# The opening of a conditioned decoder trunk: loads, folded products and the condition's spread in another order

## The chip, the cores and the metric

The kernel runs on one core of a Trainium2 chip. The core has five engines that run their own instruction streams and wait for each other by semaphores: TensorE (PE in the profile, with its weight loads as PEld), VectorE (DVE), ScalarE (ACT), GpSimd (POOL) and SyncE (SP), whose queue issues most DMAs here. The metric is the device time of one execution in microseconds (us); lower is better.

## The reference

The reference is a trunk of two layers on `x` (1 x 1024 x 1024, f32) with a condition vector `c` (1024 numbers). Each sub-layer is RMSNorm, a shift and a scale made from `c`, a mixer, a gate made from `c`, and the residual sum. The first layer's mixer projects to 2 x 2048 channels, takes trailing means over 2, 4, 8 and 16 positions minus the input, multiplies each of four groups of 512 channels by its own matrix, gates and projects back:

```python
def pool_mixer(h, w_in, w_group, scale, w_out):
    u, z = jnp.split(h @ w_in, 2, axis=-1)
    p = causal_multiscale_pool(u).reshape(B, S, N_POOL_GROUPS, GROUP_WIDTH)
    y = jnp.einsum('bsgc,gcd->bsgd', p, w_group).reshape(B, S, A_WIDTH) * scale
    return (y * jax.nn.silu(z)) @ w_out

for l in range(DEPTH):
    shift, scale, gate = jnp.split(silu(c) @ ada_w[l] + ada_b[l], 3, axis=-1)
    h = modulate(rmsnorm(x, norm_g[l]), shift, scale)
    y = mixer(h, ...)            # pooling in layer 0, windowed attention in layer 1
    x = x + gate[:, None, :] * y
return rmsnorm(x, final_g)
```

The second layer is grouped-query attention over a window of 128 positions with a shared key and value. Only the opening of the first layer is touched by the change.

## The kernel before, in words

Every f32 matrix product is made from two rounded parts of each factor, a high part (`fp32r` copy) and a low part (the factor minus its high part), in three passes: high x high, high x low, low x high. So a 128x128 by 128x512 product is three matmuls.

`x` lies transposed in SBUF as eight row blocks of 128 channels, `xk[0..7]`, each in two halves of 512 positions (`q` = 0, 1). The opening is written out by hand: inside `tc.manual_schedule` every engine runs its instructions in the order of the code. It does these things side by side:

- **Folded products** (`join_mm`, L306). For the first group the input projection and the group matrix are multiplied together first: eight blocks `m` (0 to 7), each a sum over four chunks `ci`. `fetch_c(ci)` loads the chunk's two matrices (`wgr`, and `raw` for the weights `wu`). `split_wg` makes high and low parts of `wgr` (high on ACT, L291; low on POOL, L292) and `split_wu` those of `raw` (high on ACT, low on DVE, L299 and L300). `raw` has two buffers, so the load of chunk 2 waits on SP until `split_wu(0)` is done, and that of chunk 3 until `split_wu(1)` is. Six of the eight blocks are summed in the banks `d`, `d`, `d`, `d`, `S`, `S`; blocks 6 and 7 follow in the two `S` banks once blocks 4 and 5 have left them. `joined_h` (ACT, L311) and `joined_l` (DVE, L316) turn the sums into parts.
- **Condition.** `c` lands in one row of `cact`. A product with a row of ones spreads it over 128 partitions (L434, banks `tp` and `o`); tanh on ACT (L437) and a multiply on DVE (L439) make the SiLU. `dots(k, i)` (`ada_dot`, L238) are DVE multiply-and-sum instructions: one column of shift (i = 0) or scale (i = 1) for row block `k`, from a 512 KB tile that `fetch_ada(k)` (L287) loads. There are two pairs of such tiles; `k` runs 0, 4, 1, 5, 2, 6, 3, 7.
- **Statistics.** `squares(q, ...)` on ACT (L387) and `adds(q, ...)` on DVE (L392), `fold`, then `rstd_stats` on PE: matmuls of one column (L161), `v` on DVE (L164), a power on POOL (L166), and `rstd_spread` (PE, L173), which ACT copies to `rbs[q]`.
- **First product.** `first_h(k, q)` (DVE L353, then ACT L355) and `first_l(k, q)` (DVE L359) modulate a block, and `first_mm(k, q)` (L373) multiplies it with the folded weights: twelve matmuls, eight of which need the high part and four the low part. The order is (0,0), (0,1), (4,0), (4,1), (1,0) and so on.

SP issues in this order before: chunk 0, `pk` (packed constants), `c`, chunk 1, `ada` 0, chunk 2, `x` blocks 0 to 3 of half 0, chunk 3, the other twelve half blocks of `x`, `ada` 4, and then the rest as buffers come free. Half of chunk 0's `raw` is issued on ACT's queue. After the opening a planner orders the work; the instructions there are the same, in the same order on each engine, in both kernels.

Of the kernel before, what the change touches and what calls it, by code (L numbers as in the profile page):

```python
# [18 lines left out]
P = 128  # L19
D = 1024  # L20
T = 1024
# [38 lines left out]
def trunk(ctx, tc, xT, c, pack, ada_first, ada_rest, wu0_in, wg0_in, wa, wg, wao, wkv,  # L60
# [14 lines left out]
    def bank(tag):  # L75
        return pp.tile([P, H], F32, tag=tag, name="ps_" + tag, bufs=BANKS[tag])
# [9 lines left out]
    def half(q):  # L86
        return slice(q * H, (q + 1) * H)
# [127 lines left out]
    with ExitStack() as sa:  # L215
# [18 lines left out]

        raw0 = wp.tile([P, 1024], F32, tag="raw", name="raw")
        nc.scalar.dma_start(raw0[:, half(0)], wu0_in[0, :, half(0)])
# [37 lines left out]
        def fetch_c(ci):  # L274
            nc.sync.dma_start(wgr[:, ci, :], wg0_in[ci])
            raws[ci] = wp.tile([P, 1024], F32, tag="raw", name="raw") if ci else raw0
            cols = slice(0 if ci else H, T)
            nc.sync.dma_start(raws[ci][:, cols], wu0_in[ci, :, cols])

        def fetch_x(q, ks):  # L280
            for k in ks:
                nc.sync.dma_start(xk[k][:, half(q)], xT[k * P:(k + 1) * P, half(q)])

        def fetch_ada(k):
            ads[k] = [wp.tile([P, T], F32, tag=t, name="ad") for t in ("wh", "wl")]
            for i in range(2):
                last = nc.sync.dma_start(ads[k][i], ada_first[k, :, i, :]).ins  # L287
            return last

        def split_wg(ci):  # L290
            nc.scalar.copy(out=wgs[0][:, ci, :], in_=wgr[:, ci, :])  # L291
            nc.gpsimd.tensor_sub(out=wgs[1][:, ci, :], in0=wgr[:, ci, :],  # L292
                                 in1=wgs[0][:, ci, :].bitcast(F32))

        def split_wu(ci, cols=slice(0, T), high=nc.scalar.copy):
            if len(wus) <= ci:
                wus.append(hp.tile([P, 2, T], F32R, tag="h", name="wu"))
            w = wus[ci]
            high(out=w[:, 0, cols], in_=raws[ci][:, cols])  # L299
            nc.vector.tensor_sub(out=w[:, 1, cols], in0=raws[ci][:, cols],  # L300
                                 in1=w[:, 0, cols].bitcast(F32))
# [97 lines left out]
        with tc.manual_schedule(engines={ET.PE, ET.Activation, ET.DVE, ET.Pool, ET.SP}):  # L399
            fetch_c(0)  # L400
            nc.sync.dma_start(pk, pack)
            nc.sync.dma_start(cact[0:1, :], c)
            fetch_c(1)
            fetch_ada(0)
            fetch_c(2)
            fetch_x(0, range(4))
            fetch_c(3)
            fetch_x(0, range(4, 8))
            fetch_x(1, range(8))
# [3 lines left out]
            def warm(n):  # L413

                some = ones.broadcast_to([P, P])
                for _ in range(n):
                    mm(warm_bank[:, :P], some, some, start=True, stop=True)
# [5 lines left out]
            warm(8)  # L423
            jb = [bank(t) for t in ("d", "d", "d", "d", "S", "S")]
            cbs = [bank(t) for t in ("tp", "o")]
            split_wg(0)
            split_wu(0, half(0), nc.vector.tensor_copy)
            split_wu(0, half(1))
# [4 lines left out]
            for q in range(2):  # L433
                mm(cbs[q], ones[0:1, :].broadcast_to([1, P]), cact[0:1, half(q)],  # L434
                   start=True, stop=True)
# [5 lines left out]
            join_all(1)  # L441
            split_wg(2)
            dots(0, 0, False)
            split_wu(2)
            dots(0, 1, False)
            join_all(2)
# [3 lines left out]
            split_wu(3)  # L450

# [8 lines left out]
            join_all(3, (4, 5, 0, 1, 2, 3))  # L460
            joined_h(4, 5)
            joined_l(4, 5)
            squares(1, 0, 1)
# [14 lines left out]
            jb += [bank("S") for _ in range(2)]  # L478
            for ci in range(4):
                join_mm(6, jb[6], ci)  # L480
# [4 lines left out]
            first_h(0, 0)  # L485
            rs = rstd_stats(sq2[1][0], 4, sq2[1][1])
            joined_l(6)
            first_l(0, 0)
            for ci in range(4):
                join_mm(7, jb[7], ci)  # L490
# [1471 lines left out]
```

## Time and profile before

| | |
|---|---|
| time, median of 3 runs | 963.58 us (963.45 to 964.17) |
| profiled execution, its own time | 965.07 us |
| its span, first to last instruction | 963.4 us |
| PE busy (matmuls) | 953.7 us, 99% |
| DVE busy | 757.0 us, 79% |
| ACT busy | 425.1 us, 44% |
| POOL busy | 143.7 us, 15% |
| DVE busy between 15 and 30 us | 14.96 of 15 us |
| PE busy between 0 and 90 us | 87.50 of 90 us |
| granted TensorE clock, mean | 0.997 |

Times in the views are microseconds from the start of the span. A timeline row reads: start, length, engine, line, operation, output from inputs, shape, count, and in square brackets the idle time before it with what ended that idle time. Rows merge neighbours of one kind, so a row with a count above one can hold waits inside. A row of the windows view gives for each engine its busy time and count in one stretch, then the granted clock, the DMA engines' busy share and GB/s. The line numbers are those of the kernel before; in the kernel after, the lines from 238 to 395 stand two lines earlier, and those behind the opening twelve lines later.

### The profile page before, as it was taken

Reading aid. Unit: us, or ns where it says so; the run is one execution under the profiler, and the core shown is the slowest. Engines: PE = TensorE matmul, PEld = TensorE weight load, DVE = VectorE, ACT = ScalarE, POOL = GpSimd, SP = SyncE. Lnnn points to the kernel's source line nnn. Section 1 sums busy time; section 2 is a strip of 40 time slices with the busy share of each in tenths; the row PEclk is TensorE's granted clock in tenths of the full one; section 3 lists DMA queues with packets and bytes.
Section 4 is the critical chain, followed back from the end, with each engine's and each line's share of the span. In section 5 each row is a group of like instructions: output and inputs, shape, how many; then the busy total and the mean of one; then the engine's idle time right before and its main releaser. Section 6 shows DMA issues by size and latency. Waiting matters only on the chain.

```text
span 963.4 us, 12687 instructions
## 1 busy us (share of the span) xinstructions
PE 953.7 (99%) x4468; PEld 797.0 (83%) x4468; DVE 757.0 (79%) x1414; ACT 425.1 (44%) x872; POOL 143.7 (15%) x229
## 2 busy tenths in 40 slices
PE   9999999999999999999999999999999999999997
PEld 6888888888888887888888888888888888888887
DVE  6999899686978799677755659489999757678785
ACT  6536455332533344551123335366666334455434
POOL 3000000000000000000022200222222334344521
PEclk9999999999999999999999999999999999999999
DMA  9453531354125421788888725845566543448022
GB/s 347 179 176 110 197 132 44 109 184 162 48 93 192 153 66 45 265 282 311 298 303 259 259 98 173 310 150 175 188 231 242 171 148 123 167 136 185 31 88 88
DMA packets 52081, 166.57 MB, mean 173 GB/s; under 512 B 6705, under 2 KB 7857, under 8 KB 51890
## 3 DMA queue, kind: packets, MB, share of 16 engines
q1 hardware_dynamic: 39346, 119.63, 36.0%
q0 software_dynamic: 12240, 44.57, 14.2%
q10 hardware_dynamic: 432, 1.57, 0.5%
q8 instruction: 35, 0.57, 0.2%
q14 instruction: 28, 0.23, 0.1%
HBM read 129.04 MB, written 36.70 MB: 172 GB/s over the span
## 4 chain that ended last, share of the span: by engine, by line
PE 90%; DVE 6%; DMA 2%; issue 1%; ACT 0%; DVEq 0%; ACTq 0%; SPq 0%
PE ps_d L211 12%; PE ps_d L646 11%; PE ps_d L1218 9%; PE ps_d L1219 9%; PE ps_d L1220 9%; PE ps_S L211 8%; PE ps_S L646 5%; PE ps_tp L211 4%; PE ps_tp L646 3%; PE ps_o L211 3%; PE ps_o L646 2%; DVE tmp L546 2%; PE ps_d L373 2%; PE ps_S L1355 2%; PE ps_S L1354 2%; PE ps_tp L1388 1%
## 5 line engine op out<-in xcount | busy, mean ns | idle before, releaser
L211 PE MATMUL ps_d<-gh,wh 128*128 128x512 f32 x224 | 81.9, 389 | 0.0
L238 DVE CUSTOM_DVE_ANT_0 tmp<-tmp,cact,pk 128x1024 f32<-128x1024 f32 x48 | 60.8, 1282 | 24.9 <-DMA tmp<-ada_rest 24.6
L646 PE MATMUL ps_d<-hs,ws 128*128 128x512 f32 x312 | 74.9, 389 | 0.0
L1369 ACT ACTIVATE P<-P,nm 128x129 f32<-128x129 f32 x128 | 50.2, 394 | 45.5 <-DVE nm L1365 45.3
L1218 PE MATMUL ps_d<-hm,wh 128*128 128x512 f32 x176 | 69.5, 395 | 0.0
L1219 PE MATMUL ps_d<-hm,wh 128*128 128x512 f32 x176 | 68.7, 390 | 0.0
L646 PEld LDWEIGHTS ps_d<-hs,ws 128*128 128x128 f32 x312 | 58.6, 188 | 12.1
L1220 PE MATMUL ps_d<-hm,wl 128*128 128x512 f32 x176 | 68.6, 390 | 0.0
L211 PE MATMUL ps_S<-gh,wh 128*128 128x512 f32 x192 | 67.1, 390 | 0.0
L646 PE MATMUL ps_d<-ha,ws 128*128 128x512 f32 x252 | 60.5, 389 | 0.0
L616 ACT CAST ws<-tw 128x512 fp32r<-128x512 f32 x52 | 31.9, 620 | 59.4 <-DVE tw L621 19.1
L646 PEld LDWEIGHTS ps_d<-ha,ws 128*128 128x128 f32 x252 | 47.3, 188 | 9.8
L538 POOL MEMSET tmp<- 128x16 f32 x12 | 1.3, 111 | 328.6 <-DVE adac L238 122.2
L211 PEld LDWEIGHTS ps_d<-gh,wh 128*128 128x128 f32 x224 | 42.1, 188 | 8.7
L126 ACT CAST wh<-raw 128x1024 fp32r<-128x1024 f32 x24 | 25.2, 1050 | 54.0 <-PE ps_d L211 43.8
L546 DVE TENSOR_TENSOR tmp<-tmp 128x1039 f32<-128x1039 f32 (+3 forms) x36 | 44.4, 1234 | 1.0
L211 PE MATMUL ps_d<-gh,wl 128*128 128x512 f32 x112 | 43.6, 389 | 0.0
L211 PEld LDWEIGHTS ps_S<-gh,wh 128*128 128x128 f32 x192 | 35.9, 188 | 7.4
L1431 DVE SCALAR_TENSOR_TENSOR of<-ps_o,ol 64x256 f32<-64x256 f32 x64 | 26.6, 416 | 19.5 <-ACT ol L1425 18.8
L1400 POOL TENSOR_SCALAR_AFFINE_SELECT pp<-ph 128x1024 fp32r<-128x1024 f32 x28 | 30.6, 1095 | 56.8 <-DVE ph L1393 56.7
L1220 PEld LDWEIGHTS ps_d<-hm,wl 128*128 128x128 f32 x176 | 33.0, 188 | 7.1
L1218 PEld LDWEIGHTS ps_d<-hm,wh 128*128 128x128 f32 x176 | 33.1, 188 | 6.2
(354 smaller groups left out, 2632.3 us busy)
## 6 DMA issues: line engine op xcount, KB each, us to landing
tmp<-ada_rest SPq DMA_DIRECT2D x42, 512.0 KB, 4.5
raw<-wa SPq DMA_DIRECT2D x28, 512.0 KB, 3.4
raw<-wao SPq DMA_DIRECT2D x20, 512.0 KB, 5.1
raw<-kw POOLq DMA_DIRECT2D x20, 512.0 KB, 4.4
wh<-kw POOLq DMA_DIRECT2D x19, 512.0 KB, 3.6
wl<-kw POOLq DMA_DIRECT2D x19, 512.0 KB, 4.4
ad<-ada_first SPq DMA_DIRECT2D x16, 512.0 KB, 5.5
x<-xT SPq DMA_DIRECT2D x32, 256.0 KB, 5.8
```

Source lines behind the costliest of these rows:

```text
L126: nc.scalar.copy(out=wh, in_=raw)
L211: mm(p, lhs, acts(k, hl, q), start=start and k == 0 and s == 0, stop=stop and k == n - 1 and s == 2)
L238: nc.vector.tensor_tensor_reduce(out=raw, in0=raw, in1=ca, scale=0.5, scalar=pk[:, bcol:bcol + 1], op0=ALU.mult, op1=ALU.add, accum_out=ad ...
L546: nc.vector.tensor_add(out=nx[:, 2 * s - 1:], in0=cur[:, 2 * s - 1:], in1=cur[:, s - 1:PAD + T - s])
L616: nc.scalar.copy(out=ws[i][:, 0, :], in_=src)
L646: mm(ps, lhs, acts(k, hl), start=start and k == 0 and s == 0, stop=k == 3 and s == 2, skip_group_check=True)
L1218: mm(p, lh, a[0](), start=k == 0, stop=False)
L1219: mm(p, lh, a[1](), start=False, stop=False)
L1220: mm(p, ll, a[0](), start=False, stop=k == n - 1)
L1369: note(ACT, 0.41, lambda: nc.scalar.activation(pt()[:, i, :P + 1], pt()[:, i, :P + 1], AF.Exp, bias=nm()[:, i:i + 1], scale=-1.0, accum_ou ...
L1400: note(POOL, 1.12, lambda: nc.gpsimd.affine_select(out=v8(prev()), in_=v8(cur()).bitcast(F32), pattern=[[0, 8], [-1, P]], base=-1, channel ...
L1431: note(DVE, 0.36, lambda: nc.vector.scalar_tensor_tensor(out=of()[e * 64:(e + 1) * 64, :], in0=o()[0:64, es], scalar=0.5, in1=ol()[0:64, e ...
```

## The change

Six edits, all in the opening:

1. SP's loads. The first three chunks go first, then `x` 0 to 3, chunk 3, `pk`, `x` 4 to 7, `x` 0 to 3 of half 1, then `ada` 0, then the rest of `x`, then `ada` 4. `c` moves from SP's queue to ACT's, and the half of chunk 0 that ACT's queue issued moves to SP's.
2. Chunk 0. The high part of `wgr` is made on DVE instead of ACT, and both halves of the high part of `raw` on ACT.
3. The spread of `c`. Instead of an f32 product, `c` is split on DVE into two rounded parts (`c_parts`, one row of 1024 each) and multiplied with a rounded row of ones: four `fp32r` matmuls.
4. The folded products of chunks 1, 2 and 3 go pass by pass over the six blocks, as those of chunk 0 did, instead of block by block; those of chunk 3 stand ahead of the squares in the code.
5. `dots(0, 0)` and `dots(0, 1)` move from the middle of the folding to behind `joined_l(4, 5)`.
6. Blocks 6 and 7 are summed in two pieces of six matmuls, one before and one after the sums of the statistics; and ten instead of eight f32 matmuls warm PE at the start.

```diff
-        raw0 = wp.tile([P, 1024], F32, tag="raw", name="raw")
-        nc.scalar.dma_start(raw0[:, half(0)], wu0_in[0, :, half(0)])
+        nc.scalar.dma_start(cact[0:1, :], c)
...
-        def split_wg(ci):
-            nc.scalar.copy(out=wgs[0][:, ci, :], in_=wgr[:, ci, :])
+        def split_wg(ci, high=nc.scalar.copy):
+            high(out=wgs[0][:, ci, :], in_=wgr[:, ci, :])
...
-            fetch_c(0)
-            nc.sync.dma_start(pk, pack)
-            nc.sync.dma_start(cact[0:1, :], c)
+            fetch_c(0, (half(0), half(1)))
             fetch_c(1)
-            fetch_ada(0)
             fetch_c(2)
             fetch_x(0, range(4))
             fetch_c(3)
+            nc.sync.dma_start(pk, pack)
             fetch_x(0, range(4, 8))
-            fetch_x(1, range(8))
+            fetch_x(1, range(4))
+            fetch_ada(0)
+            fetch_x(1, range(4, 8))
             fetch_ada(4)
...
-            warm(8)
+            warm(10)
...
-            split_wg(0)
-            split_wu(0, half(0), nc.vector.tensor_copy)
-            split_wu(0, half(1))
+            split_wg(0, nc.vector.tensor_copy)
+
+            c_parts = [w0[3][0:1, i].rearrange("p a t -> p (a t)") for i in range(2)]
+            c_ones = w0[2][0:1, 0, 0, :P]
+            nc.vector.tensor_copy(out=c_ones, in_=ones[0:1, :].broadcast_to([1, P]))
+            nc.vector.tensor_copy(out=c_parts[0], in_=cact[0:1, :])
+            nc.vector.tensor_sub(out=c_parts[1], in0=cact[0:1, :], in1=c_parts[0].bitcast(F32))
+            for cols in (half(0), half(1)):
+                split_wu(0, cols)
...
             for q in range(2):
-                mm(cbs[q], ones[0:1, :].broadcast_to([1, P]), cact[0:1, half(q)],
-                   start=True, stop=True)
+                for i in range(2):
+                    mm(cbs[q], c_ones, c_parts[i][:, half(q)], start=i == 0, stop=i == 1)
...
-            join_all(1)
+            for i in range(3):
+                join_all(1, s=(i,))
             split_wg(2)
-            dots(0, 0, False)
             split_wu(2)
-            dots(0, 1, False)
-            join_all(2)
+            for i in range(3):
+                join_all(2, s=(i,))
...
             split_wu(3)
+            joined_order = (4, 5, 0, 1, 2, 3)
+            for i in range(3):
+                join_all(3, joined_order, (i,))
...
-            join_all(3, (4, 5, 0, 1, 2, 3))
             joined_h(4, 5)
             joined_l(4, 5)
+            dots(0, 0, False)
+            dots(0, 1, False)
+            jb += [bank("S") for _ in range(2)]
+            for ci in range(2):
+                join_mm(6, jb[6], ci)
...
-            jb += [bank("S") for _ in range(2)]
-            for ci in range(4):
+            for ci in range(2, 4):
                 join_mm(6, jb[6], ci)
...
             first_h(0, 0)
+            for ci in range(2):
+                join_mm(7, jb[7], ci)
             rs = rstd_stats(sq2[1][0], 4, sq2[1][1])
             joined_l(6)
             first_l(0, 0)
-            for ci in range(4):
+            for ci in range(2, 4):
                 join_mm(7, jb[7], ci)
```

How the instructions stand now, at three places. First DVE from the start of the data to the first `adds`: before, where `ISA ad` is a dot.

```order
L299 CAST wu<-raw 128x512
L300 TENSOR_TENSOR wu<-raw,wu 128x512 x2
L300 TENSOR_TENSOR wu<-raw,wu 128x1024
L439 SCALAR_TENSOR_TENSOR cact<-cact,ps_tp 128x512
L439 SCALAR_TENSOR_TENSOR cact<-cact,ps_o 128x512
L238 ISA ad,adac<-ad,cact,pk 128x1024
L238 ISA adac 128x1
L300 TENSOR_TENSOR wu<-raw,wu 128x1024
L238 ISA ad,adac<-ad,cact,pk 128x1024
L238 ISA adac 128x1
```

And now the same stretch of DVE, where `w_128` holds the row of ones and `w_129` the two parts of `c`:

```order
L289 CAST wgs<-wgr 128x512
L428 CAST w_128<-ones 1x128
L429 CAST w_129<-cact 1x1024
L430 TENSOR_TENSOR w_129<-cact,w_129 1x1024
L298 TENSOR_TENSOR wu<-raw,wu 128x512 x2
L298 TENSOR_TENSOR wu<-raw,wu 128x1024
L443 SCALAR_TENSOR_TENSOR cact<-cact,ps_tp 128x512
L443 SCALAR_TENSOR_TENSOR cact<-cact,ps_o 128x512
L298 TENSOR_TENSOR wu<-raw,wu 128x1024
```

Three instructions for `c` now stand ahead of the low part of chunk 0, and the two dots have left the stretch; they stand behind the two `joined_l` rows of blocks 4 and 5 (`ps_S`). Second, SP's queue before:

```order
L275 DMA wgr<-wg 128x512
L278 DMA raw<-wu 128x1024
L287 DMA ad<-ada_first 128x1024 x2
L275 DMA wgr<-wg 128x512
L278 DMA raw<-wu 128x1024
L282 DMA x<-xT 128x512 x4
```

and now, from chunk 1 to the end of `x`:

```order
L276 DMA raw<-wu 128x1024
L280 DMA x<-xT 128x512 x4
L273 DMA wgr<-wg 128x512
L276 DMA raw<-wu 128x1024
L403 DMA pk<-pack 128x128
L280 DMA x<-xT 128x512 x8
L285 DMA ad<-ada_first 128x1024 x2
L280 DMA x<-xT 128x512 x4
```

The 1 MB of `ada` 0 no longer stands between chunks 1 and 2 but behind twelve of the sixteen half blocks of `x`. Third, PE around the sums of the statistics before, where L161 is the sums, L173 the spread and L306 on `ps_S` the blocks 6 and 7:

```order
L161 MATMUL ps_o<-invd,first 128x1 x4
L306 MATMUL ps_S<-wgs,wu 128x512 x12
L173 MATMUL ps_tp<-ident,rs 128x128 x4
L161 MATMUL ps_o<-invd,second 128x1 x8
L306 MATMUL ps_S<-wgs,wu 128x512 x12
```

and now:

```order
L304 MATMUL ps_S<-wgs,wu 128x512 x6
L161 MATMUL ps_o<-invd,first 128x1 x4
L304 MATMUL ps_S<-wgs,wu 128x512 x6
L173 MATMUL ps_tp<-ident,rs 128x128 x4
L304 MATMUL ps_S<-wgs,wu 128x512 x6
L161 MATMUL ps_o<-invd,second 128x1 x8
L304 MATMUL ps_S<-wgs,wu 128x512 x6
```

Each block of twelve matmuls now stands as six before and six after a group of sums.

More of the change, by code (lines that the diff above doesn't have):

```diff
@@ L272, in trunk, with fetch_c @@
         raws, ads = {}, {}
-        def fetch_c(ci):
+        def fetch_c(ci, parts=(slice(0, T),)):
             nc.sync.dma_start(wgr[:, ci, :], wg0_in[ci])
-            raws[ci] = wp.tile([P, 1024], F32, tag="raw", name="raw") if ci else raw0
-            cols = slice(0 if ci else H, T)
-            nc.sync.dma_start(raws[ci][:, cols], wu0_in[ci, :, cols])
+            raws[ci] = wp.tile([P, 1024], F32, tag="raw", name="raw")
+            for cols in parts:
+                nc.sync.dma_start(raws[ci][:, cols], wu0_in[ci, :, cols])
         def fetch_x(q, ks):
@@ L288, in fetch_ada, with split_wu @@
             return last
-        def split_wg(ci):
-            nc.scalar.copy(out=wgs[0][:, ci, :], in_=wgr[:, ci, :])
+        def split_wg(ci, high=nc.scalar.copy):
+            high(out=wgs[0][:, ci, :], in_=wgr[:, ci, :])
             nc.gpsimd.tensor_sub(out=wgs[1][:, ci, :], in0=wgr[:, ci, :],
                                  in1=wgs[0][:, ci, :].bitcast(F32))
-        def split_wu(ci, cols=slice(0, T), high=nc.scalar.copy):
+        def split_wu(ci, cols=slice(0, T)):
             if len(wus) <= ci:
@@ L298, in split_wu @@
             w = wus[ci]
-            high(out=w[:, 0, cols], in_=raws[ci][:, cols])
+            nc.scalar.copy(out=w[:, 0, cols], in_=raws[ci][:, cols])
             nc.vector.tensor_sub(out=w[:, 1, cols], in0=raws[ci][:, cols],
```

## The prediction

> **What bounds the kernel now.** I read the page's busy times first, then the windows view, then the timelines of PE and DVE in the first 50 us, the chain of waits there, and the DMA issues.
>
> ```profile
> PE 953.7 (99%) x4468; PEld 797.0 (83%) x4468; DVE 757.0 (79%) x1414; ACT 425.1 (44%) x872; POOL 143.7 (15%) x229
> ...
> 81.50:300.00 218.50, 218.50 (x964) 180.56 (x963) 184.31 (x267) 91.97 (x158) 0.89 (x8) 1.00 0.38 130
> 300.00:600.00 300.00, 299.56 (x1330) 247.96 (x1329) 218.50 (x310) 108.33 (x162) 16.85 (x33) 1.00 0.60 206
> 600.00:900.00 300.00, 300.00 (x1506) 253.21 (x1505) 237.02 (x628) 157.01 (x421) 98.49 (x143) 1.00 0.56 183
> ```
>
> From 81.5 to 900 us PE is idle 0.44 us. What the opening saves or loses therefore reaches the end whole; the rest does not change. The question is what lets PE out of the opening.
>
> ```profile
> 25.85 1.28 DVE L392 TENSOR_TENSOR second<-second,tmp 128x512 f32<-128x512 f32 x2
> ...
> 30.72 1.28 DVE L316 TENSOR_TENSOR w<-ps_d,w 128x512 fp32r<-128x512 f32 x2
> ...
> 37.39 0.69 DVE L316 TENSOR_TENSOR w<-ps_S,w 128x512 fp32r<-128x512 f32 x1 [0.78 <-ACT w L311]
> 38.28 0.75 DVE L353 SCALAR_TENSOR_TENSOR x<-x,acol,second 128x512 f32<-128x512 f32 x1 [0.20 <-ACT second L495]
> 39.83 0.75 DVE L359 SCALAR_TENSOR_TENSOR a<-x,adac,a 128x512 fp32r<-128x512 f32 x1 [0.79 <-ACT a L355]
> ...
> 44.23 0.74 DVE L359 SCALAR_TENSOR_TENSOR ha<-x,adac,ha 128x512 fp32r<-128x512 f32 x1
> ```
>
> ```profile
> 44.32 0.67 DVE ha L359
> ...
> 45.03 1.21 PE ps_d L373 x4
> ```
>
> DVE runs without a stop up to 36.61 and then waits 0.78, 0.20 and 0.79 us. The chain of waits enters PE's stream from `first_l(4, 0)` (DVE, 44.23): PE needs that low part for the last four matmuls of (4,0) and gets it at 45.03. So **DVE's list, not PE's, lets PE out of the opening**, and the end moves as `first_l(4, 0)` moves. After that PE leads:
>
> ```profile
> 48.84 2.88 PE L373 MATMUL ps_d<-ha,w 128*128 128x512 f32 x12
> 51.56 0.39 PE L373 MATMUL ps_tp<-a,w 128*128 128x512 f32 x1
> ```
>
> Twelve matmuls take 51.56 - 48.84 = 2.72 us, 0.227 each, 5.44 for the two halves of a block; DVE needs two dots (1.20 each) and four modulations (0.665 each), 5.06.
>
> PE has a loss of its own, which edit 6 aims at:
>
> ```profile
> 31.00:32.00 1.00, 1.00 (x11) 1.00 (x10) 1.00 (x3) 0.02 (x1) 0.00 (x0) 0.96 0.00 0
> 32.00:33.00 1.00, 1.00 (x5) 0.90 (x5) 1.00 (x4) 0.30 (x1) 0.19 (x1) 0.50 0.00 0
> ...
> 35.00:36.00 1.00, 1.00 (x5) 0.82 (x4) 1.00 (x3) 0.00 (x0) 0.00 (x0) 0.83 0.00 0
> ```
>
> ```profile
> 30.35 2.12 PE L161 MATMUL ps_o<-invd,second 128*128 128x1 f32 x16 [0.44 <-DVE second L392]
> 32.33 4.41 PE L306 MATMUL ps_S<-wgs,wu 128*128 128x512 f32 x12
> ```
>
> The third number from the right is the granted clock: half speed from about 31.9 to 35.3, so 1.7 us of PE work lost, behind 2.12 us of one-column sums. Block 7 takes 4.41 where twelve take 2.72. Of this DVE feels the waits of 0.78 and 0.20 (block 7's parts, then `rbs[1]`).
>
> [...]
>
> **The change part by part.** Warm-up: 16 instructions take 3.76, so four more end at 5.70; the first product starts 0.44 later than its 5.26.
>
> ```profile
> 1.00 3.76 PE L417 MATMUL ps_S<-ones 128*128 128x128 f32 x16 [1.00 <-DVE ones L103]
> ...
> 4.69 0.43 DVE L299 CAST wu<-raw 128x512 fp32r<-128x512 f32 x1 [3.68 <-DMA raw<-wu]
> 5.15 2.40 DVE L300 TENSOR_TENSOR wu<-raw,wu 128x512 fp32r<-128x512 f32 x2
> 5.22 3.47 POOL L292 TENSOR_TENSOR wgs<-wgr,wgs 128x512 fp32r<-128x512 f32 x2 [3.35 <-ACT wgs L291]
> 5.26 1.17 PE L306 MATMUL ps_d<-wgs,wu 128*128 128x512 f32 x4 [0.50 <-ACT wgs L291]
> 7.05 1.19 PE L306 MATMUL ps_d<-wgs,wu 128*128 128x512 f32 x4 [0.17 <-POOL wgs L292]
> 7.58 0.33 SPq L278 DMA_DIRECT2D raw<-wu  x1
> 8.55 1.07 PE L306 MATMUL ps_d<-wgs,wu 128*128 128x512 f32 x4
> 10.00 1.12 PE L434 MATMUL ps_tp<-cact,ones 1*128 1x512 f32 x2
> 11.91 3.02 PE L306 MATMUL ps_d<-wgs,wu 128*128 128x512 f32 x12
> 13.20 1.30 POOL L292 TENSOR_TENSOR wgs<-wgr,wgs 128x512 fp32r<-128x512 f32 x1 [4.50 <-ACT wgs L291]
> 13.37 2.21 DVE L238 CUSTOM_DVE_ANT_0 ad<-ad,cact,pk 128x1024 f32<-128x1024 f32 x1
> 13.39 1.05 ACT L299 CAST wu<-raw 128x1024 fp32r<-128x1024 f32 x1 [0.27 <-DMA raw<-wu]
> 16.65 1.27 DVE L238 CUSTOM_DVE_ANT_0 ad<-ad,cact,pk 128x1024 f32<-128x1024 f32 x1
> 17.85 2.38 DVE L392 TENSOR_TENSOR first<-first,tmp 128x512 f32<-128x512 f32 x2
> 17.91 1.05 ACT L299 CAST wu<-raw 128x1024 fp32r<-128x1024 f32 x1 [0.62 <-DMA raw<-wu]
> 20.16 1.21 DVE L300 TENSOR_TENSOR wu<-raw,wu 128x1024 fp32r<-128x1024 f32 x1
> 21.96 1.28 ACT L311 CAST w<-ps_S 128x512 fp32r<-128x512 f32 x2 [0.84 <-PE ps_S L306]
> ```
>
> Nothing hides that 0.44 but PE's own wait for POOL at 7.05: `wgr`, now first and alone on its queue, should land near 3.8 instead of 4.5 (estimate: the two first loads shared the pipe), so POOL's low part is ready at about 6.2 and the second pass starts at 7.06, as before.
>
> **`c` on DVE** is the main cost. No row shows a DVE instruction on one partition. Per partition 1024 numbers are read, so the nearest rows are the 0.43 copy of 512 (some 0.7 for 1024) and the 1.21 subtraction of 1024; with the row of ones 2.1 us. The lower end is nothing. I take the upper one, since DVE's rows go by numbers per partition (0.69 against 1.21 for 512 and 1024). And it collides: a dot that takes 1.27 took 2.21 while POOL's subtraction ran from 13.20 to 14.50, and POOL's two took 3.47 instead of 2.6, so each waits for the other to end. In turn: `wgr` high to 4.25, ones and copy to 5.0, POOL to 6.2, `c`'s subtraction to 7.4, POOL's second to 8.55, the two low parts of chunk 0 to 9.2 and 9.85 (before: 5.8 and 7.55). The third pass of chunk 0 then starts at 9.36 instead of 8.55, with 0.93 us of idle PE ahead of it.
>
> [...]
>
> The spread itself gets shorter: 10.00 to 11.91 before, now four matmuls, 0.91. Chunk 1 starts at 9.36 + 6 x 0.227 + 0.91 = 11.63, 0.28 earlier.
>
> **Loads.** SP's load of chunk 2's `raw` waits for the low part of chunk 0: issued at 9.9, not 7.58. Before, `ada` 0 filled the pipe meanwhile; now it drains. On an empty pipe 512 KB land after 3.2 us:
>
> ```profile
> ad<-ada_first SPq DMA_DIRECT2D x1, 512.0 KB, 3.2
> ```
>
> (the issue of `ada` 1 at 35.46). That gives 13.1, against 13.39 before: the delay and the removed 1 MB cancel. From there 1.75 MB landed up to 17.91, 0.646 per 256 KB. So chunk 3's `raw` comes at 17.7, eight half blocks of `x` and `pk` by 23.0, `ada` 0 at 24.3 and 25.6, the last `x` at 28.2.
>
> **Pass by pass.** Chunks 1 to 3 are 54 matmuls, 12.26 us; from 11.63 PE meets no wait (low parts at 11.0, 15.6, 20.0, needed at 14.35, 18.4, 22.5) and ends at 23.9 instead of 25.2. But blocks 4 and 5, which before finished first in chunk 3, now finish in its third pass: `joined_h(4)` starts at 11.63 + 49 x 0.227 + 0.2 = 23.0, not 21.96. `joined_l(4, 5)` run 23.65 to 24.85.
>
> **The dots** then run 24.85 to 27.25 (the second tile has landed at 25.6). So the `adds` of half 1 start at 27.25 instead of 25.85: **+1.40**. Their `x` is not the limit: the last lands at 28.2, wanted at 30.9. ACT's squares start 1.0 later, not 1.4, and stay ahead of DVE.
>
> **From there to `first_l(4, 0)`** DVE's list is the same, 44.23 - 25.85 = 18.38 with the three waits. PE: the `adds` end at 32.1, the sums (second half of 2.12) at 33.5, the power (1.01) and `v` at 34.8, six fillers at 35.0, the spread at 36.2, ACT's copy at 36.9; DVE reaches `first_h(0, 1)` at 38.6. So the waits of 0.78 and 0.20 go: **-0.98**. The 0.79, for ACT inside block (0,1), stays. Sum: 1.40 - 0.98 = **+0.42 us**, span 963.4 + 0.4 = 963.8. The profiled execution took 965.07, 1.5 over the median of 963.58; the same shift on the median gives **964.0 us**. PE's savings (1.7 of clock, 1.0 in the spread) end as PE waiting for DVE at (0,1) and (4,0).
>
> **The rivals.** About 0.2%, 1.9 us, is what a measurement of this kernel tells from no change.
>
> A, *`c` costs little* or does not collide. Then chunk 0's low parts are not late, PE runs unbroken from 5.70 and blocks 4 and 5 are out 0.9 to 1.0 earlier than I reckon, and so is everything behind. -0.9 + 0.4 = -0.5 to -0.9 us: 962.7 to 963.1. For it: one partition; against: the row rate.
>
> B, *PE led after all*, and the gain arrives: `first_mm` starts not at 37.38 but two us sooner, and DVE follows because its three waits (1.77) and the one at POOL (two `adds` took 2.38 at 17.85, 1.28 at 25.85) all go: -2.0 to -2.9, 960.7 to 961.6. Against: the dots still cannot start before 24.3.
>
> C, on the other side, *the condition's load decides*. DVE takes instructions in order, and behind the second dot queue all `adds`, `joined_l` and `first_h`, and so both of PE's last sums. From a landing of `ada` 0's second tile after 26.05 each us counts in full. If the drained pipe resumes slowly (5 to 10 us moved 324 GB/s, later 408, a fifth less, over the 5.3 MB between 9.9 and 25.6), it lands 2.5 to 3.4 later, 0.45 of it in the slack; with the +0.42 that is +2.4 to +3.4, 966.0 to 967.0.
>
> ```profile
> 5.00:10.00 5.00, 4.57 (x18) 3.22 (x18) 3.51 (x4) 2.44 (x4) 3.47 (x2) 1.00 0.97 324
> 10.00:15.00 5.00, 5.00 (x19) 3.22 (x19) 3.20 (x4) 3.31 (x6) 1.30 (x1) 1.00 1.04 408
> ```
>
> D, *the clock drops again*, elsewhere: the fillers do not do what they are for. PE idles 1.7 us before the first spread (27.9 to 29.8, waiting for POOL) and sums follow. A half-speed stretch of 3.4 us costs PE 1.7; at 31.9 it would delay the second spread by 1.2 past its slack: +1.6, 965.2. Ahead of 24 us it would cost 1.7 whole, +2.1, 965.7.
>
> **How the numbers follow.** My sum 0.50 (964.0, its own range 963.3 to 964.9), A 0.15, B 0.10, C 0.12, D 0.13. Range: down to A's lower end with 0.4 beyond it, 962.3; past D's upper end to where C begins, 966.0; outside lie B and most of C, 0.2. Faster by over 0.2%: B, 0.10. Slower: C and the upper half of D, 0.18. Within: 0.72.
>
> **What would show it.** Right: DVE L429 and L430 last 0.7 and 1.2 or more; SP's third `raw` is issued near 9.9; the first dot starts behind 24; PE's clock stays 1.00 from 28 to 36; PE waits for DVE before (0,1) and inside (4,0). Wrong: L430 under 0.5; a dot that waits for its DMA; `first_l(4, 0)` more than 1 us from 44.6; or PE idle time behind 50 us that was not there before.

## The result, and the profile after

The changed kernel takes 966.50 us (median of 10 runs, 965.73 to 971.07), the kernel before 963.92 (10 runs, 963.25 to 965.05): a ratio of 1.0029, interval 1.0019 to 1.0039, or **2.6 us slower**. The forecast was 964.0, with a range to 966.0. The profiled execution took 966.25 us, its span is 964.5.

The page of the kernel after, PE's and DVE's busy time:

```profile
PE 951.5 (99%) x4472; PEld 796.0 (83%) x4472; DVE 756.8 (78%) x1417; ACT 425.5 (44%) x872; POOL 143.2 (15%) x229
```

PE is busy 2.2 us less than before, and yet the kernel is slower: the loss is not in PE's own work but in what PE waits for. DVE's timeline of the kernel after, in the opening:

```profile
4.15 0.68 DVE L429 CAST w<-cact 1x1024 fp32r<-1x1024 f32 x1
4.86 2.19 DVE L430 TENSOR_TENSOR w<-cact,w 1x1024 fp32r<-1x1024 f32 x1
6.97 1.27 DVE L298 TENSOR_TENSOR wu<-raw,wu 128x512 fp32r<-128x512 f32 x2
...
24.89 1.28 DVE L236 CUSTOM_DVE_ANT_0 ad<-ad,cact,pk 128x1024 f32<-128x1024 f32 x1 [0.88 <-DMA ad<-ada_first]
...
27.35 1.29 DVE L390 TENSOR_TENSOR second<-second,tmp 128x512 f32<-128x512 f32 x2
...
44.58 0.74 DVE L357 SCALAR_TENSOR_TENSOR ha<-x,adac,ha 128x512 fp32r<-128x512 f32 x1
```

The first dot starts at 24.89 (forecast 24.85), `adds` of half 1 at 27.35 (27.25), `first_l(4, 0)` at 44.58 (44.65). PE's timeline there, and the granted clock (third number from the right of the windows view):

```profile
29.87 1.16 PE L173 MATMUL ps_tp<-ident,rs 128*128 128x128 f32 x8 [2.46 <-POOL rs L166]
...
45.38 1.19 PE L371 MATMUL ps_d<-ha,w 128*128 128x512 f32 x4 [0.35 <-DVE ha L357]
```

```profile
31.00:32.00 1.00, 1.00 (x6) 0.81 (x5) 1.00 (x3) 0.93 (x2) 0.00 (x0) 1.00 0.88 361
...
33.00:34.00 1.00, 1.00 (x11) 1.00 (x11) 1.00 (x2) 0.00 (x0) 0.00 (x0) 1.00 0.01 4
```

So this execution's opening is 0.35 us later than that of the execution shown before (45.38 against 45.03), at full clock, close to the 0.42 of the forecast. A second loss follows far behind it:

```profile
341.09 0.69 DVE L633 TENSOR_TENSOR tw<-raw 128x512 f32<-128x512 f32 x1 [1.07 <-DMA raw<-wa]
...
379.22 0.50 PE L211 MATMUL ps_d<-p,wh 128*128 128x512 f32 x1 [0.80 <-ACT p L578]
```

A load landed late at 341 us, and PE lost 1.2 us behind it at 380. The opening's 0.3 us has been made up by 150 us, so this loss alone makes the 1.1 us between the two spans; but the medians are 2.6 apart. So these two executions do not stand for the two kernels.

### The profile page after: what moved, and what is told of

Read it like the earlier page. It is cut to its first block, busy times and chain, and to the rows that moved or that the text cites. A ratio compares the mean times of both kernels' runs of the same rounds, so it can differ in the third digit from the quotient of the medians.

```text
span 964.5 us, 12694 instructions
## 1 busy us (share of the span) xinstructions
PE 951.5 (99%) x4472; PEld 796.0 (83%) x4472; DVE 756.8 (78%) x1417; ACT 425.5 (44%) x872; POOL 143.2 (15%) x229
## 4 chain that ended last, share of the span: by engine, by line
PE 90%; DVE 6%; DMA 2%; issue 1%; SPq 0%; ACT 0%; DVEq 0%; ACTq 0%
PE ps_d L211 12%; PE ps_d L658 11%; PE ps_d L1230 9%; PE ps_d L1231 9%; PE ps_d L1232 9%; PE ps_S L211 8%; PE ps_S L658 5%; PE ps_tp L211 4%; PE ps_o L211 3%; PE ps_tp L658 3%; PE ps_o L658 2%; PE ps_d L371 2%; PE ps_S L1367 2%; PE ps_S L1366 2%; DVE tmp L558 2%; PE ps_tp L1400 1%
## 5 line engine op out<-in xcount | busy, mean ns | idle before, releaser
L628 ACT CAST ws<-tw 128x512 fp32r<-128x512 f32 x52 | 31.9, 620 | 60.2 <-DVE tw L633 21.3
L1412 POOL TENSOR_SCALAR_AFFINE_SELECT pp<-ph 128x1024 fp32r<-128x1024 f32 x28 | 30.6, 1095 | 56.7 <-DVE ph L1405 56.7
L211 PE MATMUL ps_d<-p,wh 128*128 128x512 f32 x96 | 37.6, 392 | 1.3 <-ACT p L578 0.8
```

Source lines behind the costliest of these rows:

```text
L211: mm(p, lhs, acts(k, hl, q), start=start and k == 0 and s == 0, stop=stop and k == n - 1 and s == 2)
L628: nc.scalar.copy(out=ws[i][:, 0, :], in_=src)
L1412: note(POOL, 1.12, lambda: nc.gpsimd.affine_select(out=v8(prev()), in_=v8(cur()).bitcast(F32), pattern=[[0, 8], [-1, P]], base=-1, channel ...
```

## The experiments

Two measures serve throughout. **The ratio** of a kernel's time to that of the kernel before on the same chip. And **the start of block (1,0)** on PE, the row that stands at 48.84 in the profile before: from there to 110 us PE runs without a wait, so it is the opening's length (the runs with an added tile, below, apart). It comes from one execution of each kernel, the ratio from 5 to 12.

| run | ratio (interval) | median, us | start of (1,0) | half clock in the opening |
|---|---|---|---|---|
| before, as shown | 1 | 963.92 | 48.84 | 31.9 to 35.3 |
| before_again | 1.0000 (0.9992 to 1.0009) | 964.79 | 48.70 | 31.9 to 35.3 |
| warm10 | 1.0026 (1.0012 to 1.0041) | 967.09 | 47.81 | 12.3 to 15.7 |
| pad8 | 1.0018 (0.9998 to 1.0037) | 967.17 | 47.44 | 11.9 to 15.3 |
| fill_only | 1.0021 (1.0009 to 1.0033) | 966.65 | 48.68 | 12.2 to 15.6 |
| fill_warm8 | 0.9997 (0.9983 to 1.0012) | 966.18 | 48.24 | none |
| after, as shown | 1.0029 (1.0019 to 1.0039) | 966.50 | 49.14 | none |
| after_again | 1.0036 (1.0024 to 1.0048) | 968.31 | 50.63 | 30.6 to 34.0 |
| after_warm8 | 1.0020 (1.0003 to 1.0038) | 966.61 | 49.27 | none |
| dense | 1.0022 (1.0010 to 1.0033) | 966.48 | 49.56 | none |
| ada_sooner | 1.0030 (1.0017 to 1.0043) | 967.46 | 48.52 | none |
| sooner_warm8 | 1.0007 (0.9995 to 1.0020) | 966.59 | 48.39 | none |
| c_f32 | 1.0038 (1.0025 to 1.0051) | 968.55 | 51.47 | 13.2 to 16.6 |
| ada_back | 1.0062 (1.0049 to 1.0075) | 969.90 | 51.58 | 21.5 to 24.9 |
| before_row2 | 0.9999 (0.9990 to 1.0008) | 964.71 | 47.40 | none |
| after_row2 | 1.0014 (1.0005 to 1.0024) | 966.44 | 51.24 | 31.0 to 34.4 |

### Both kernels again

No edit. 

> The kernel before, unchanged, for a second trace. Theory 1 (the shown execution was not typical): its stretch of half clock from 31.9 to 35.3 us is not in every execution, and where it is missing DVE does not wait 0.78 and 0.20, and the last four matmuls of (4,0) start about 1.0 us earlier than 45.03. Then the typical span is 962.0 to 962.4, and the changed kernel loses 1.4 us in the opening alone. Theory 2 (the opening is as shown, the loss lies behind it): the second trace has the same half clock and the matmuls at 45.0, give or take 0.1, and the 1 us between this execution and the median comes from somewhere behind 50 us.

> The changed kernel, unchanged, for a second trace. Both theories: the last four matmuls of (4,0) near 45.4, clock 1.00 up to 48 us, median near 966.4. Theory 2 needs the load that landed late at 341 us (4.6 us after its issue, with DVE waiting 1.07) and PE's waits of 0.80 and 0.53 at 380 us here too. If they are missing and the span is near 963.4, the late load is an accident of one execution; if some executions show a mean clock of 0.996 or less and a span over 966, there are further half-clock stretches.

The kernel before has the half clock at the same place again (windows view of before_again):

```profile
32.00:33.00 1.00, 1.00 (x4) 0.90 (x4) 1.00 (x3) 0.41 (x1) 0.29 (x1) 0.50 0.00 0
```

So theory 1 seemed to fall; later runs brought it back (below). The changed kernel, though, now has a half clock too, from 30.6 to 34.0, against both theories. Its windows and DVE's wait behind them:

```profile
28.00:29.00 1.00, 0.08 (x1) 0.00 (x0) 1.00 (x4) 1.00 (x4) 0.15 (x1) 1.00 1.04 426
29.00:30.00 1.00, 0.06 (x1) 0.07 (x1) 1.00 (x3) 1.00 (x4) 0.88 (x1) 1.00 1.01 414
...
31.00:32.00 1.00, 1.00 (x5) 0.90 (x4) 1.00 (x3) 0.49 (x2) 0.00 (x0) 0.50 0.84 344
```

```profile
35.78 0.16 DVE L164 TENSOR_SCALAR v<-ps_o 128x4 f32<-128x4 f32 x1 [1.55 <-PE ps_o L161]
```

PE waits for POOL's power (the first two rows), the clock halves, the sums of half 1 come late, and DVE waits 1.55 for them. That is rival D, at the price I gave it (+1.6). The load at 341 us is on time here. It is late again in fill_only and in after_row2 (DVE waits 0.92 and PE loses 1.0 at 380 in each), and in no other trace: it comes and goes with the execution, and all three kernels have ten warm-ups.

### Parts of the change, undone or alone

fill_only is the kernel before with edit 6 alone. 

> The kernel before with edit 6 alone (blocks 6 and 7 in two pieces around the sums, ten warm-up matmuls). Theory 1: if the half clock is rare, the fillers have nothing to repair and cost what they delay: 0.3 to 0.8 us slower than before, 964.2 to 964.8. Theory 2: the half clock is in every execution, DVE's waits of 0.98 go, and the kernel is 0.3 to 1.0 us faster, 962.9 to 963.6. Clock 1.00 from 30 to 36 us in both.

ada_back is the changed kernel with edit 5 undone, and of edit 1 the place of `ada` 0's load:

```diff
             fetch_c(1)
+            fetch_ada(0)
             fetch_c(2)
...
             split_wg(2)
+            dots(0, 0, False)
             split_wu(2)
+            dots(0, 1, False)
```

> The changed kernel with edits 1 (the place of ada 0's load) and 5 undone together: the condition's first tiles between chunks 1 and 2 again, the two dots in the middle of the folding. The rest is the changed kernel. If the dots behind joined_l(4, 5) and the late load are what costs, adds of half 1 start at 25.9 to 26.3 instead of 27.35 and the time falls by 1.0 to 1.4 to 965.0 to 965.4. If it is chunk 0's late low parts and the pass-by-pass order, chunk 2 and 3 come later now (ada 0 stands in the queue ahead of them, 1.6 us of it behind the late issue) and the time stays or rises by 0.4, 966.4 to 966.9. If the loss lies behind 50 us, the opening's time changes but the total does not follow it.

Edit 6 alone made the kernel before 0.21% slower (2.0 us), more than either theory allowed, with an opening no longer than the one shown before; in its trace PE loses 1.0 us at 380, behind the late load. ada_back was the worst of all: with `raw` of chunk 2 issued late and 1 MB of `ada` ahead of it in the queue, PE waits for chunk 2's low part,

```profile
20.36 1.20 PE L304 MATMUL ps_d<-wgs,wu 128*128 128x512 f32 x4 [1.87 <-DVE wu L298]
```

and the clock halves there as well. So with the rest of the change in place, undoing the move of the dots gains nothing.

### Dense filler, an earlier load, the old spread, two warm-ups

In after_again the half clock came behind PE's wait before the first spread. dense fills that wait with products nobody reads:

```diff
+            for _ in range(10):
+                mm(jb[7], wus[0][:, 0, :P], wgs[0][:, 0, :], start=True, stop=True)
             gain_col(0)
```

> The changed kernel with ten more 128x512 products on PE that compute nothing that is used, behind the second piece of block 6, where PE waits 2.5 us for POOL before the first spread (they end about 0.5 us before the spread). [...] Theory S (DVE's later list alone: dots at 24.9 instead of 13.4): no change, 2.6 to 3.8 us over the kernel before.

ada_sooner: `fetch_ada(0)` ahead of `fetch_x(1, range(8))`. 

> The changed kernel with ada 0 loaded ahead of all of half 1 of x instead of behind four of its blocks. Theory S: the dots are bound by their load (DVE waits 0.88 for it at 24.9), so the first dot starts at 24.0, adds of half 1 at 26.5 instead of 27.35, and the time falls by 0.9 us. [...] If x 0 to 3 of half 1, now landing 2.6 us later, hold up ACT's squares, the adds wait and nothing is gained.

c_f32: edits 2 and 3 undone. 

> The changed kernel with edits 2 and 3 undone: c spread by an f32 product, high part of wgr on ACT, that of raw's first half on DVE. Theory S with my step on c (2.1 us of DVE at the start cost 0.9 us of PE): low parts of chunk 0 at 5.8 and 7.0, raw of chunk 2 issued by 7.6, but the spread takes 1.9 instead of 0.9; sum between -0.5 and +0.7 us against the changed kernel. [...]

warm10: in the kernel before, `warm(10)` for `warm(8)`, nothing else. 

> The kernel before with ten instead of eight warm-up matmuls and nothing else, since before with all of edit 6 took 2.1 us more. If the two warm-ups delay the first product (by 0.44 us) and that is most of the loss, 0.4 us slower or more. If the loss comes from PE's instruction fetches, which eight more PE instructions move by 1 us against the loads of the middle (a 16 KB packet of the instruction queue fell into the load that DVE waits for at 340 us), DVE waits about 0.9 us there and the kernel is 0.5 to 1.2 us slower, with nothing lost before 50 us. If the split of blocks 6 and 7 is the cause, this kernel equals the one before within 0.4 us.

dense kept the clock at 1.00 (windows view):

```profile
27.00:30.00 3.00, 3.00 (x14) 2.45 (x14) 3.00 (x8) 3.00 (x7) 1.03 (x1) 1.00 1.03 421
30.00:33.00 3.00, 3.00 (x21) 2.62 (x19) 3.00 (x7) 1.65 (x4) 0.00 (x0) 1.00 0.67 272
```

but its ratio, 1.0022, is within the interval of the changed kernel's: a gain from the full clock is not shown. ada_sooner took DVE's wait for the load away:

```profile
24.28 1.28 DVE L236 CUSTOM_DVE_ANT_0 ad<-ad,cact,pk 128x1024 f32<-128x1024 f32 x1
...
26.69 1.29 DVE L390 TENSOR_TENSOR second<-second,tmp 128x512 f32<-128x512 f32 x2
```

`adds` at 26.69 instead of 27.35, the opening 0.62 shorter than as shown, and the time was no better either. Something outside the opening weighs too: at 880 us PE lost 2.0 us in dense's trace and 1.0 in ada_sooner's. c_f32 has the half clock early, from 13.2 to 16.6; its opening is among the longest, and its time no better. warm10 showed the place best. It differs from the kernel before in two f32 matmuls on PE (four of the rows counted as matmuls, 4472 for 4468), the order of everything else is the same, its opening is 1.0 us *shorter* than as shown, and it is 2.5 us slower, more than any of its cases allowed. Its loss is at 880 us. ACT and PE of warm10 there, then ACT of the kernel before:

```profile
882.62 1.06 ACT L1676 CAST wo<-raw 128x1024 fp32r<-128x1024 f32 x1 [8.64 <-DMA raw<-wbo]
...
888.19 0.47 PE L1418 MATMUL ps_o<-pp,VS 128*128 128x512 f32 x1 [3.45 <-DVE of L1431]
```

```profile
878.54 1.05 ACT L1676 CAST wo<-raw 128x1024 fp32r<-128x1024 f32 x1 [3.40 <-DMA raw<-wbo]
```

A wait of up to some 4 us costs PE nothing there (3.40 in the kernel before, 4.01 and 3.93 in two traces of the changed one); the 8.64 cost it 5.9, with the half clock that followed (its offset to the kernel before goes from -1.2 at 860 us to +4.8 at 910). This execution took 969.86, 2.8 over warm10's own median, so it is a bad case. In the other eight traces with 4472 matmuls or more ACT waited 2.7 to 6.0, and PE lost 0 to 2.0. Of the five with 4468, two lost as well: fill_warm8 1.6 and sooner_warm8 1.4.

### Eight or ten warm-ups

In the trace of the kernel before the instruction queue's packets of 16 KB come some 29 us apart up to 600 us (21 from 25.1 to 599.7), which is 128 matmuls of 0.227 us. With two warm-ups more each should fall elsewhere. Four kernels told the count from the rest: after_warm8 and sooner_warm8 (the changed kernel and ada_sooner with `warm(8)`), fill_warm8 (fill_only with it), and pad8 (the kernel before with two one-column matmuls elsewhere):

```diff
             jb += [bank("S") for _ in range(2)]
+            for _ in range(2):
+                mm(jb[7][:, :1], ones.broadcast_to([P, P]), ones[:, :1], start=True, stop=True)
```

> The changed kernel with eight instead of ten warm-ups, so PE has 4468 matmuls as before, not 4472. Theory F (the place in PE's program where its instruction fetches fall): two more warm-ups alone made the kernel before 2.7 us slower, all of it in a wait for raw<-wbo at 880 us, with the fetch of the instruction queue at 872 instead of 887. If that is the loss of the changed kernel too, it is 0.0 to 0.8 us from the kernel before here, its times lie closer together, the trace has no fetch between 871 and 880, and ACT waits under 4 us for raw<-wbo. Theory O (the opening): the opening of the changed kernel costs what it costs, 2.0 us or more over before stay.

> The kernel before with two one-column matmuls that compute nothing used, into the free bank ahead of block 6, where PE has idle time later: 4472 matmuls, warm-up as before. Theory F: as with the two warm-ups, 1.5 to 2.7 us slower than before with widely spread times, the fetch at 872 to 874 and a wait for raw<-wbo over 4 us. If the warm-up itself (its length, or the first product 0.4 us later) is what costs, this kernel equals the one before within 0.4 us.

> The kernel before with the split of blocks 6 and 7 around the sums and eight warm-ups: 4468 matmuls. Theory F: the 2.1 us of edit 6 come from its two warm-ups, so this is between 0.6 faster and 0.3 slower than before. If the split costs, 1 us slower or more.

> The changed kernel with eight warm-ups and ada 0 ahead of all of half 1 of x. Theory F with the opening as the traces show it (DVE's wait of 0.88 for ada gone): 0.5 faster to 0.4 slower than the kernel before. Theory O: 2 us slower or more.

By the ratios the number of PE's instructions seems to count, not the warm-up: 1.0026, 1.0018 and 1.0021 for the opening of the kernel before or nearly so with 4472 matmuls (warm10, pad8, fill_only), 1.0000 and 0.9997 with 4468 (before_again, fill_warm8). This is not shown, though. pad8's interval touches 1, and the four runs of this section share a chip on which the kernel before itself took 963.27 to 969.69, with a median of 965.62 (964.36 and 964.49 on the chips of warm10 and fill_only), so that a ratio of 0.9997 does not say that the wait is gone. sooner_warm8 came down from 1.0030 to 1.0007, with intervals that overlap. after_warm8 stayed at 1.0020, above the 0.0 to 0.8 us expected: theory F explains a part at most. And the place of the fetch is not the cause by itself: fill_warm8's trace has it at 889, late as in the kernel before (887), and ACT waited 5.6 us all the same; sooner_warm8, with 4468 matmuls too, has it at 874.

### The store beside the load

What holds `raw<-wbo` up? SP issues a store of 1024 single numbers, `row<-adac` (1024 packets of 4 bytes), right behind it. In warm10 the two were issued within 1 us, and each needed 13.7 us (the DMA view; KB and us to landing):

```profile
raw<-wbo SPq DMA_DIRECT2D x1, 512.0 KB, 13.7
...
row<-adac SPq DMA_DIRECT2D x1, 4.0 KB, 13.7
```

though the last 4 KB packet of the load had been moved by 875. Held back behind ACT's last `wo<-raw` by a copy on ACT:

```diff
+        gates = tile_of("gates", sp, [P, 8], F32, 1)
+        note(ACT, 0.2, lambda: nc.scalar.copy(out=gates(), in_=adac[:, 40:48]),
+             last_w[3][0].on, [(gates, 0)])
         note(SP, 0.35, lambda: nc.sync.dma_start(
-            row.rearrange("n p -> p n"), adac[:, 40:48]), last_w[3][0].on, [(at, 0)], 4.0)
+            row.rearrange("n p -> p n"), gates()), [(gates, 0)], [(at, 0)], 4.0)
```

> The kernel before with the 4 KB store row<-adac made from a copy that ACT makes behind its last wo<-raw, so that the store cannot run beside the load of raw<-wbo. Theory R (the store's 1024 packets of 4 bytes hold up the landing of the load): ACT waits under 1.5 us for raw<-wbo at 875, the store is issued at 876 to 878, and the times lie close together at 963.4 to 964.2; no PE wait near 885. If the place of the instruction fetch is the cause by itself, wait and spread stay as before.

> The changed kernel with the store held back in the same way. Theory R: what is left over the kernel before with the store held back is the opening and the load at 340 us: 0.3 to 1.5 us, 964.2 to 965.4, and no time over 968. Theory O (the opening costs the 2.5 us): 2 us or more over it.

> The kernel before with ten warm-ups and the store held back. Theory R: the 2.7 us of the two warm-ups vanish: within 0.5 us of the kernel before with the store held back, times close together, though the fetch falls at 872 here as well. If the fetch is the cause by itself, 1.5 us or more over it.

> The changed kernel with ada 0 ahead of all of half 1 of x and the store held back. Theory R with the opening bound by DVE's list: 0.5 to 0.9 us faster than the changed kernel with the store held back, so -0.5 to +0.6 against the kernel before with it. If x of half 1 comes late, no faster.

All four were 9 to 13 us slower than the kernel before, for a reason of their own (the last section). Among themselves they answer: before_row 974.17 us (973.76 to 974.56) and warm10_row 974.04 (973.65 to 975.06). With the store held back, **the two warm-ups cost nothing** that four runs of each can show; the slow matmuls had moved PE by some 8 us there, so the loads met another schedule as well. after_row took 977.33 and soon_row 975.10, which is 3.2 and 0.9 over before_row where 0.3 to 1.5 and -0.5 to +0.6 were expected; after_row's trace has the half clock from 31.2 to 41.5.

before_row2 and after_row2 copy into `asch`, a tile that exists and is not read any more, so that no address moves. 

> The kernel before with the store row<-adac held back, its source in a tile that exists already. If the new tile slowed the matmuls, PE's offset to the kernel before stays constant from 50 to 860 us and the time is 963.3 to 964.2 with all runs within 2 us, 0.3 to 1.2 us below the kernel before on the same chip; ACT waits under 1.5 us for raw<-wbo. If holding the store back is itself what slows the kernel, 973 to 974 again.

> The changed kernel with the store held back in the same way. What it is over the kernel before with the store held back is the opening and the load at 340 us: 1.0 to 2.5 us by the traces so far (best executions 1.6 apart with the new tile; an opening offset of 0.3 to 1.8 against an execution of the kernel before that had itself lost 1 us to half clock), so 964.5 to 966.5. My forecast's own size, +0.42, would give 963.8 to 964.6.

The timelines of ACT and SP of before_row2:

```profile
873.93 2.00 ACT L1679 CAST wo<-raw 128x1024 fp32r<-128x1024 f32 x2
...
876.05 0.39 SPq L1533 DMA_DIRECT2D row<-asch  x1
```

Its DMA view, the load's landing and the packets, MB and share of POOL's queue from 871 to 880 us; then the same queue and stretch of the kernel before:

```profile
raw<-wbo SPq DMA_DIRECT2D x1, 512.0 KB, 4.3
...
q0 software_dynamic: 288, 1.05, 34.7%
```

```profile
q0 software_dynamic: 64, 0.26, 38.0%
```

The wait is gone, the load lands after 4.3 us, and POOL's queue moves 1.05 MB in the 9 us in which it moved 0.26 beside the store. Of the fourteen traces that have the store right behind the load, the load needed 7.7 to 13.7 us in thirteen; in before_again it needed 4.3 there too, and ACT did not wait. So the store goes with the late landing, but does not force it. From 130 us on PE's offset is now constant: the slow matmuls came with the added tile. The time of the kernel before does not change (0.9999, where 0.3 to 1.2 us less was expected), which fits a wait that is seldom over the 4 us of slack; that of the changed kernel falls from 1.0029 and 1.0036 to 1.0014. The intervals of 1.0036 (from 1.0024) and 1.0014 (to 1.0024) just meet, and the two traces of the changed kernel with the store in place, where ACT waited 4.01 and 3.93, lost nothing at 880 us. That half of the loss lies there is a reading from the times, not a proof.

before_row2 also shows the opening of the kernel before without half clock. Windows, DVE, PE:

```profile
32.00:33.00 1.00, 1.00 (x6) 0.83 (x6) 1.00 (x3) 0.55 (x1) 0.44 (x1) 1.00 0.00 0
```

```profile
25.59 1.28 DVE L392 TENSOR_TENSOR second<-second,tmp 128x512 f32<-128x512 f32 x2
...
38.42 0.75 DVE L359 SCALAR_TENSOR_TENSOR a<-x,adac,a 128x512 fp32r<-128x512 f32 x1 [0.79 <-ACT a L355]
42.82 0.75 DVE L359 SCALAR_TENSOR_TENSOR ha<-x,adac,ha 128x512 fp32r<-128x512 f32 x1
...
43.63 1.20 PE L373 MATMUL ps_d<-ha,w 128*128 128x512 f32 x4 [0.35 <-DVE ha L359]
```

The wait of 0.79 is there; those of 0.78 and 0.20 are not. The changed kernel's `adds` start 27.35 - 25.59 = 1.76 later and its last matmuls of (4,0) 45.38 - 43.63 = 1.75 later, behind the same wait of 0.35. None of the kernels tried is faster than the kernel before; sooner_warm8 and fill_warm8 are not told from it.

## Why the prediction was wrong

- **DVE's list lets PE out of the opening: right.** 1.76 at the `adds` and 1.75 at (4,0), in executions at full clock.
- **+1.40 for the `adds`: right in size** (27.35 - 25.85 = 1.50), but by luck, since two errors in the steps to it cancel. The times for `c` were right: its copy took 0.68 and the subtraction 2.19, from 4.86 on, beside POOL's L290 (4.18 to 5.97). That a subtraction of one row would stand in turn with POOL, on which the steps up to 9.85 rest, no run had shown; this 2.19, where 1.2 was reckoned without POOL, is what the changed kernel shows of it. But the low parts ran 6.97 to 8.24, not 8.55 to 9.85, and `raw` of chunk 2 was issued at 8.28, not 9.9. What that gained was taken by the load: DVE waited 0.88 for `ada` 0, the dot that waits for its DMA which I had named as a sign of error.
- **-0.98 for the waits of 0.78 and 0.20: the step that failed.** That the fillers of edit 6 would keep the clock up, no run had shown; in the profiled execution of the changed kernel the clock over them is 1.00, in after_again it is at half from 30.6 to 34.0 over the same fillers. The waits do vanish, but they belong to an execution with half clock from 31.9 to 35.3. Of seven openings of the kernel before (warm10, pad8 and the runs with the store held back counted), two have it and start block (1,0) at 48.70 and 48.84, with both waits (0.78 and 0.77, 0.20 and 0.20); five do not, have neither wait and start it at 47.40 to 47.93. I had the hint: the profiled execution took 965.07, 1.5 above the median. I carried the sum over to the median as "the same shift"; that shift was, in good part, the very loss I booked as the change's gain. The mean clocks of the executions fit: of the 29 of the kernel before that ran beside warm10, nine have the 0.997 of the two traces, and their median is 964.93; that of the other twenty is 964.04. Without the gain my own sum gives +1.4, 965.0. With the 0.36 by which the `adds` were too small against an opening at full clock (1.76), that is 1.3 of the 2.2 us missed.
- **Rival D: right as a mechanism, but it does not hold the median.** Three of five openings of the changed kernel lost at least one stretch to half clock near 31 us (starts of (1,0) at 50.63, 51.24 and, in after_row, 52.26; without it 49.14 and 49.27). Not the length of PE's wait for POOL decides it: with 2.46 the clock stayed full, with 1.82 to 1.86 it halved. But each execution's mean granted clock is on record, and in all 20 traces it is 0.998 or more where the clock is full up to 950 us and 0.997 or less where it is not. By that, eight of the ten executions behind the result had no half clock, and their median is 966.25, still 2.3 over the kernel before; of all 27 executions of the changed kernel, after_again and after_row2 it is 19. In the kernel before such stretches are commoner, in 76 of the 117 executions beside the experiments; near 12 us they cost its opening little (warm10 and pad8 start (1,0) at 47.81 and 47.44).
- **"The rest does not change", and what the opening loses "reaches the end whole": failed too.** I took it from one execution in which PE is idle 0.44 us from 81.5 to 900. In others PE loses 0.5 to 1.5 us at 127 (three traces), 1.0 to 1.2 at 380 (three) and 0.4 to 5.9 at 880 (eight). So a load at 880 us that often uses up its 4 us of slack was in no step, and the two warm-ups were priced only where they are issued (their 0.44 us is hidden, as forecast). These stops also take gains back: before_row2 loses 1.2 of its 1.4 at 127 us,

```profile
127.47 3.03 PE L646 MATMUL ps_tp<-hs,ws 128*128 128x512 f32 x12 [1.03 <-ACT ps_o L657]
```

  while pad8 and warm10 keep theirs up to 870.
- **How much each share weighs** is settled in part. The mean start of (1,0) is 48.0 in the seven openings of the kernel before and 50.5 in the five of the changed one, but three of those five have the half clock, so that mean says too much. With the store held back, the executions with a mean clock of 0.998 or more have medians of 964.48 (five of before_row2) and 966.37 (nine of after_row2): 1.9 us with neither half clock nor store, near the 1.75 at (4,0). The other 0.7 of the 2.6 stays open between the half clock and the load at 880 us; the late load at 341 can be in either part. Open too is what decides how long the load waits beside the store, and whether PE's instruction count has a part in it.

## What to carry to other kernels

Before crediting a change with a wait that it removes, look whether the wait is in every execution: a profiled execution above the median is a warning, and a second trace of the *kernel before* is the cheapest experiment. Use the clock that is recorded for every execution to see whether a trace is typical. Look at the clock behind a wait of PE as well: behind one of 1.82 to 1.86 us for POOL, three of five openings of the changed kernel had half clock, the one with 2.46 us had none (dense, which filled that wait, stayed at 1.00, though without a gain that its ratio shows). And look for a load that lands within a few microseconds of its need, next to a store of single numbers: here, behind two more warm-ups, ACT waited 8.64 us for one at 880 us, and PE lost 5.9.

## What the hardware showed that was not expected

**In the openings the half clock lasts 3.41 us or three times that, and begins at no fixed place.** In the trace of the kernel before, it is at half from 31.92 to 35.33, 3.41 us, behind 27.31 us on record at full clock and ahead of 925.01, which are 8 and 271 times as long (from 960.34 it is at half to the end); in that of the kernel after, the full clock lasts 955.73 us, 280 times. In the other openings with a half clock it lasts 3.4 us too (the table above), in after_row 10.3, three times as long. Where it begins differs from execution to execution: at 30.6 in after_again, 31.0 in after_row2 and 31.2 in after_row, all of them with the opening of the changed kernel. The prediction carried 31.9 to 35.3 over from one execution. The 3.41 us up to the drop in the kernel before (28.50 to 31.92) hold three matmuls of 128x512, 0.52 us, beside products of 128x128 and one-column sums, with PE busy 2.98 us in all; 28.46 to 31.87 in the kernel after hold five, 1.09 us, with PE busy 2.00, and the clock stays at 1.00. So of these two it fell where the 128x512 products were fewer, though PE was the busier. How many of them keep it up is not shown.

**32 bytes more per partition slowed PE's matmuls.** With the tile `gates`, twelve matmuls of a block took longer all along; before_row, then the row of the kernel before:

```profile
47.93 2.96 PE L373 MATMUL ps_d<-ha,w 128*128 128x512 f32 x12
...
53.45 1.80 PE L373 MATMUL ps_d<-ha,w 128*128 128x512 f32 x7
```

```profile
54.28 2.88 PE L373 MATMUL ps_d<-ha,w 128*128 128x512 f32 x12
```

From 47.93 to 53.45 are 5.52 us for a block; before, 48.84 to 54.28, 5.44. Over the kernel this came to 9 us. That the copy went into an old tile without this cost (before_row2) shows that the tile did it; that it is the addresses behind it was not tried.

**A 4 KB store of single numbers takes 11 to 15 us, and a load beside it mostly lands late.** The store took 11.4 to 15.0 us in fourteen traces. In warm10 the load beside it had its packets through by 875 and landed at 882.6, and ACT waited 8.64 us for it. The load needed 7.7 to 13.7 us in thirteen of the fourteen; in before_again it was not late (4.3). Why the store takes so long is not shown.
